# A two-layer encoder on one core: the first projection of each mixer has its weights split 1024 columns at a time instead of 512

## The chip, the cores and the metric

The kernel runs on one core of a Trainium2 chip. The metric is the device time of one execution in microseconds (us), lower is better; the figure for a kernel is the median of its runs.

## What is computed

256 tokens of width 1024 go through two layers. Each layer is a half-weighted SwiGLU feed-forward, a mixer, and a second feed-forward, each added to the stream:

```python
for layer in range(DEPTH):                       # DEPTH = 2
    h = rms_norm(x, ffn1_norm[layer])
    x = x + 0.5 * swiglu(h, ffn1_w_gate[layer], ffn1_w_up[layer], ffn1_w_down[layer])
    h = rms_norm(x, mix_norm[layer])
    if layer % 2 == 0: x = x + even_mixer(h, ...)
    else:              x = x + odd_mixer(h, ...)
    h = rms_norm(x, ffn2_norm[layer])
    x = x + 0.5 * swiglu(h, ffn2_w_gate[layer], ffn2_w_up[layer], ffn2_w_down[layer])
return rms_norm(x, final_norm)
```

The even mixer makes one projection of 1536 columns: queries, keys and values of `a` (8 query heads, 2 key heads, global attention with normed queries and keys and a two-axis rotation) and of `b` (the same sizes, a window of 128 tokens, a one-axis rotation, a sink). The odd mixer projects to queries, keys and values of 16 heads of 64 and attends in a neighbourhood with a learned bias. Each mixer ends with an output projection. All inputs and outputs are float32.

## The kernel before

The program is written out as one ordered list of instructions: each engine (PE, ScalarE = ACT, VectorE = DVE, GpSimd = POOL, SyncE = SP) executes its instructions in the order in which the Python code issues them. There are six stages, numbered 0 to 5: feed-forward, even mixer, feed-forward, feed-forward, odd mixer, feed-forward.

**Weights.** A weight block is loaded by SP as float32 into one of a few `raw` buffers (128x4x512 or 128x2x1024). On the chip it is cut into a high part and a low part of the narrower float type fp32r: `hi` is a copy on ACT (line 482, `high_part`), `lo` is raw minus `hi` on DVE (line 485, `low_part`). Activations are cut in the same way (`th`, `tl`; `oT..h`, `oT..l`; `qTb`, `kTbz` and so on, on the same two lines). A product of 512 columns is then three matmuls: high by high (L474), low by high (L475), high by low (L476).

**Splits.** One raw block becomes two `Split` objects of two pieces of 512 columns each. `Split.step` says how many pieces one `hi` and one `lo` instruction treat: one if the split is `narrow` (128x512), otherwise both (128x1024). The fifth entry that a unit of the plan yields (`"narrow"` or `"wide"`) sets this. The split tiles of weights come from a pool of seven pairs of 128x2x512.

**Order.** After each group of three matmuls `mm` calls `tick`:

```python
def tick(self, supply=True):
    self.low()                        # the lo of the split part whose hi was issued last
    for task in list(self.tasks): ... # small tasks: softmax, transposes, rotations
    if supply:
        self.due += self.rate
        n = self.whole[0].step() if self.whole else 1
        if self.due >= n and self.room():
            self.due = min(self.due - n, n)
            self.supply()             # one hi of the next split, on ACT
```

So `hi` and `lo` of weights to come are strewn between the small tasks of the mixer, at a rate per projection (`EVEN_RATE`, `ODD_RATE`), and a wide split is issued when twice as much is due. The splits issued while one projection is multiplied are those of weights used later. A task counts ticks of `mm`, and the waits between its steps are numbers in tables. A load of the next raw block is issued with the last `lo` of a block.

**The tasks around the change.** In the even mixer, `keys` (L1195 to L1206) turns a key block on PE into a `tp` bank of PSUM (two banks in turn), from which `kTaz`/`kTbz` (ACT, high) and `kTax`/`kTbx` (DVE, low) are made. `queries` rotates on DVE (`t` L1144, `qr` L1157), turns `qr` on PE into the next `tp` bank (L552), and makes `qTb` highs on ACT (L482), then lows on DVE (L485). Scores are matmuls on lines 1068 and 1069, maxima L1081, exponentials `p` L1108, their transposes L1130, copies `pt` L1028, value products `o` L1053. The output projection multiplies `oTa10h`, `oTa10l` (even) or `ot_12h`, `ot_12l` (odd) with split weights, and L617 adds the result to `x`.

Of the kernel before, what the change touches and what calls it, by code (L numbers as in the profile page):

```python
# [21 lines left out]
D = 1024  # L22
# [175 lines left out]
def pairs(stage):  # L198
    return [({"p": "plain", "s": "strassen"}[o[0]], int(o[1:])) for o in DOWN[stage].split()]
# [9 lines left out]
class Trunk:  # L209
# [88 lines left out]
    def plan(self):  # L298


        a = self.a

        def columns(w2d, spans, units=None, kind="narrow"):
            w = sum(n for _, n in spans)
            k = 0
            for nk in units or (4, 4):
                pieces, o = [], 0
                for c0, n in spans:
                    src = w2d[k * P : (k + nk) * P, c0 : c0 + n].rearrange("(k p) n -> p k n", p=P)
                    pieces.append(((slice(0, P), slice(0, nk), slice(o, o + n)), src))  # L310
                    o += n
                yield pieces, nk, w, [2], kind
                k += nk

        def ffn(n, l, stage):
            c0 = 0
            for ci, w in enumerate(FF_CHUNKS):
                first = stage == 0 and c0 == 0
                if ci in SEVEN[stage]:
                    for k in range(0, KD, 2):  # L320
                        pieces = []
                        for i, name in enumerate(("_w_gate", "_w_up")):
                            src = a[n + name][l][k * P : (k + 2) * P, c0 : c0 + w].rearrange("(k p) n -> p k n", p=P)
                            pieces.append(((slice(0, P), slice(0, 2), slice(i * w, i * w + w)), src))
                        yield pieces, 2, D, [2], "strassen" if k >= KD - 2 * SEVEN[stage][ci] else "wide"
                    c0 += w
                    continue
                yield from columns(a[n + "_w_gate"][l], [(c0, w)], FIRST if first else None, "narrow" if first else "wide")
                yield from columns(a[n + "_w_up"][l], [(c0, w)], None, "wide")
                c0 += w  # L330
            for k in range(0, KD, 4):
                pieces = []
                for i, name in enumerate(("_w_gate", "_w_up")):
                    src = a[n + name][l][k * P : (k + 4) * P, c0 : c0 + FF_MIXED].rearrange("(k p) n -> p k n", p=P)
                    pieces.append(((slice(0, P), slice(0, 4), slice(i * FF_MIXED, (i + 1) * FF_MIXED)), src))
                yield pieces, 4, 2 * FF_MIXED, [2], "wide"
            for i, (kind, pair) in enumerate(pairs(stage)):
                src = a[n + "_w_down"][l][2 * pair * P : 2 * (pair + 1) * P, :].rearrange("(k p) n -> p k n", p=P)
                uses = [2, 3 if stage == 5 and i >= len(pairs(stage)) - HELD else 2]
                yield [(slice(0, P), src)], 2, D, uses, "wide" if kind == "plain" else kind  # L340

        def even():
            w_in, w_out = a["even_w_in"][0], a["even_w_out"][0]
            for spans in ([(512, 256), (1280, 256)], [(768, 512)], [(0, 512)]):
                yield from columns(w_in, spans)
            for g in (1, 0):
                for nh in range(2):
                    pieces = []
                    for s in range(2):
                        r0 = g * 512 + s * 256  # L350
                        src = w_out[r0 : r0 + 256, nh * 512 : nh * 512 + 512].rearrange("(j p) n -> p j n", p=HD)
                        pieces.append((slice(64 * s, 64 * s + 64), src))
                    yield pieces, 4, 512, [2], "narrow"

        def odd():
            w_qkv, w_out = a["odd_w_qkv"][0], a["odd_w_out"][0]
            for g in range(2):
                for i in (1, 0, 2):
                    yield from columns(w_qkv, [(i * D + g * 512, 512)])
            for g in range(2):  # L360
                for nh in range(2):
                    src = w_out[g * 512 : g * 512 + 512, nh * 512 : nh * 512 + 512].rearrange("(j p) n -> p j n", p=P)
                    yield [(slice(0, P), src)], 4, 512, [2], "narrow"

        yield from ffn("ffn1", 0, 0)
        yield from even()
        yield from ffn("ffn2", 0, 2)
        yield from ffn("ffn1", 1, 3)
        yield from odd()
        yield from ffn("ffn2", 1, 5)  # L370

# [1207 lines left out]
```

## Time and profile before

| | |
|---|---|
| median of 3 runs | 936.25 us (936.07 to 936.27) |
| the profiled execution | 935.71 us |
| its span on the core | 933.7 us, so 2.0 us lie around it |
| granted TensorE clock | 0.999 of full speed |
| `lo` (L485) and `hi` (L482) of weights | 372 each, 377.7 us on DVE and 320.1 us on ACT |

The even mixer's projections, attention and output projection lie between 180 and 280 us of the span, the odd mixer's between 620 and 760. In the rows of the timeline the first number is the start and the second the time for all instructions of the row; a bracket at the end is how long the engine stood idle before, and for whom. In the windows, numbers follow as busy time and count of PE, weight loads, DVE, ACT and POOL, then the granted clock, the DMA share and GB/s.

### The profile page before, as it was taken

What the parts mean: (1) busy time and instruction counts of PE and PEld (TensorE: products, weight loads), DVE (VectorE), ACT (ScalarE), POOL (GpSimd) and SP (SyncE); (2) the same over time, 40 slices, a digit from 0 to 9 for tenths busy, and PEclk for the clock granted to TensorE, in tenths of its full rate; (3) what the DMA queues carried; (4) which work ended last, traced back from release to release, by engine and by line L of the source; (5) the groups of instructions that cost most, each with busy time, mean ns of one, the idle gap of its engine ahead of it and who ended that gap; (6) DMA issues with size and microseconds to landing.
All of it is one profiled execution on the core that took longest, in us unless ns stands there. A gap on an engine that the chain in (4) does not pass through costs nothing.

```text
span 933.7 us, 12374 instructions
## 1 busy us (share of the span) xinstructions
PE 921.5 (99%) x4405; PEld 754.3 (81%) x4405; DVE 773.4 (83%) x1198; ACT 675.9 (72%) x1084; POOL 92.6 (10%) x152
## 2 busy tenths in 40 slices
PE   9999999999999999999999999999999999999997
PEld 6887888877778888888888888888878888888885
DVE  6799679778868889799878888978867696977898
ACT  7778876467777778885657879657777586778853
POOL 1300000064420000000100000008030000000001
PEclk9999999999999999999999999999999999999999
DMA  8857865644327577757466787566434367588651
GB/s 297 283 172 256 244 213 184 218 142 109 112 92 231 173 237 236 233 191 265 156 193 211 216 278 207 225 210 200 155 99 159 105 204 225 168 265 254 164 212 53
DMA packets 129341, 183.14 MB, mean 196 GB/s; under 512 B 50688, under 2 KB 63744, under 8 KB 129280
## 3 DMA queue, kind: packets, MB, share of 16 engines
q1 hardware_dynamic: 128704, 181.58, 61.8%
q8 instruction: 34, 0.56, 0.2%
q10 hardware_dynamic: 576, 0.79, 0.2%
q14 instruction: 27, 0.22, 0.1%
HBM read 169.76 MB, written 1.05 MB: 183 GB/s over the span
## 4 chain that ended last, share of the span: by engine, by line
PE 88%; DVE 7%; ACT 3%; issue 1%; POOL 0%; POOLq 0%; ACTq 0%; DVEq 0%
PE s L476 13%; PE s L475 13%; PE s L474 12%; PE pj L474 12%; PE pj L475 11%; PE pj L476 11%; DVE lo L485 3%; PE o L474 2%; PE o L476 2%; PE o L475 2%; PE o L1053 2%; PE tp L1130 1%; ACT hi L482 1%; PE tp L530 1%; PE tp L474 1%
## 5 line engine op out<-in xcount | busy, mean ns | idle before, releaser
L485 DVE TENSOR_TENSOR lo<-raw,hi 128x1024 fp32r<-128x1024 f32 (+1 forms) x372 | 377.7, 1034 | 81.8 <-ACT hi L482 80.2
L482 ACT ACTIVATE hi<-raw 128x1024 fp32r<-128x1024 f32 (+1 forms) x372 | 320.1, 892 | 53.9 <-PE s L476 12.6
L474 PE MATMUL s<-hi,th 128*128 128x512 f32 x378 | 148.1, 392 | 0.0
L475 PE MATMUL s<-lo,th 128*128 128x512 f32 x378 | 147.2, 389 | 0.2 <-DVE lo L485 0.2
L476 PE MATMUL s<-hi,tl 128*128 128x512 f32 x378 | 147.2, 390 | 0.0
L474 PE MATMUL pj<-hi,th 128*128 128x512 f32 x366 | 146.2, 399 | 0.0
L475 PE MATMUL pj<-lo,th 128*128 128x512 f32 x366 | 143.2, 391 | 0.6 <-DVE lo L485 0.4
L476 PE MATMUL pj<-hi,tl 128*128 128x512 f32 x366 | 142.8, 390 | 0.0
L475 PEld LDWEIGHTS s<-lo,th 128*128 128x128 f32 x378 | 71.0, 188 | 15.0 <-DVE lo L485 0.5
L476 PEld LDWEIGHTS s<-hi,tl 128*128 128x128 f32 x378 | 70.9, 188 | 14.9
L474 PEld LDWEIGHTS s<-hi,th 128*128 128x128 f32 x378 | 71.0, 188 | 14.5
L475 PEld LDWEIGHTS pj<-lo,th 128*128 128x128 f32 x366 | 68.9, 188 | 15.2 <-DVE lo L485 2.6
L476 PEld LDWEIGHTS pj<-hi,tl 128*128 128x128 f32 x366 | 68.7, 188 | 14.5
L474 PEld LDWEIGHTS pj<-hi,th 128*128 128x128 f32 x366 | 68.8, 188 | 14.0 <-issue 1.0
L494 POOL TENSOR_TENSOR rstd<-var,mhalf 128x1 f32<-128x1 f32 (+2 forms) x16 | 17.1, 1070 | 586.6 <-ACT th L515 309.7
L563 ACT COPY turned<-glu 128x1024 uint16<-128x1024 uint16 (+1 forms) x48 | 60.2, 1253 | 13.2 <-DMA glu<-turned 13.2
L559 ACT COPY turned<-glu 128x1024 uint16<-128x1024 uint16 (+1 forms) x48 | 46.3, 965 | 24.1 <-DVE glu L797 16.3
L482 ACT ACTIVATE shi<-raw 128x1024 fp32r<-128x1024 f32 x28 | 29.6, 1059 | 32.7 <-DVE raw L398 23.0
L474 PE MATMUL s<-hi,g_h 128*128 128x512 f32 (+1 forms) x134 | 52.5, 392 | 0.0
L476 PE MATMUL s<-hi,g_l 128*128 128x512 f32 (+1 forms) x134 | 52.0, 388 | 0.0
L475 PE MATMUL s<-lo,g_h 128*128 128x512 f32 (+1 forms) x134 | 52.0, 388 | 0.0
L482 ACT ACTIVATE shi<-two 128x1024 fp32r<-128x1024 f32 x28 | 29.6, 1058 | 23.8 <-DVE two L398 23.7
(350 smaller groups left out, 1657.3 us busy)
## 6 DMA issues: line engine op xcount, KB each, us to landing
raw<-in_ffn_w_down SPq DMA_DIRECT2D x44, 1024.0 KB, 5.1
raw<-in_ffn_w_up SPq DMA_DIRECT2D x28, 1024.0 KB, 5.1
raw<-in_ffn_w_gate SPq DMA_DIRECT2D x26, 1024.0 KB, 5.3
raw<-in_ffn_w_gate SPq DMA_DIRECT2D x35, 512.0 KB, 4.2
raw<-in_ffn_w_up SPq DMA_DIRECT2D x32, 512.0 KB, 5.2
raw<-in_odd_w_qkv SPq DMA_DIRECT2D x12, 1024.0 KB, 5.2
raw<-in_even_w_in SPq DMA_DIRECT2D x4, 1024.0 KB, 5.1
raw<-in_even_w_out SPq DMA_DIRECT2D x8, 512.0 KB, 5.7
```

Source lines behind the costliest of these rows:

```text
L474: mm(ps, h, wh, start=first, stop=False)
L475: mm(ps, h, wl, start=False, stop=False)
L476: mm(ps, l, wh, start=False, stop=last)
L482: self.nc.scalar.activation(hi, src, AF.Copy)
L485: self.nc.vector.tensor_tensor(lo, src, hi.bitcast(F32), op=ALU.subtract)
L494: nc.gpsimd.tensor_tensor(r[:, :n], v[:, :n], self.mhalf[:, :n], op=ALU.pow)
L530: nc.tensor.transpose(tb[:, j * P : (j + 1) * P], self.x[tt][:, b * P : (b + 1) * P], self.ident)
L559: self.nc.scalar.copy(planes.rearrange("p (h c) -> p h c", h=2), back.rearrange("p (c h) -> p h c", h=2))
L563: self.nc.scalar.copy(planes.rearrange("p (c h) -> p h c", h=2), back.rearrange("p (h c) -> p h c", h=2))
L1053: self.nc.tensor.matmul(O[64 * s : 64 * s + 64, i * P : i * P + P], v(b0 + i, s, kc), pT[s][:, i, kc, :], start=(kc == 0), stop=(kc == 1),)
L1130: nc.tensor.transpose(tb[:, o : o + P], p[:, i, kc * P : kc * P + P], self.ident)
```

## The change

The first projection of each mixer (in the even mixer the keys and values of `a` and `b`, 512 columns in all; in the odd mixer the first keys) gets the kind `"wide"`: its four splits are made by one `hi` and one `lo` of 128x1024 each, instead of two and two of 128x512. The others stay narrow.

```diff
         def even():
             w_in, w_out = a["even_w_in"][0], a["even_w_out"][0]
-            for spans in ([(512, 256), (1280, 256)], [(768, 512)], [(0, 512)]):
-                yield from columns(w_in, spans)
+            for spans, kind in (([(512, 256), (1280, 256)], "wide"), ([(768, 512)], "narrow"), ([(0, 512)], "narrow")):
+                yield from columns(w_in, spans, None, kind)
...
             for g in range(2):
                 for i in (1, 0, 2):
-                    yield from columns(w_qkv, [(i * D + g * 512, 512)])
+                    yield from columns(w_qkv, [(i * D + g * 512, 512)], None, "wide" if (g, i) == (0, 1) else "narrow")
```

PE's and POOL's instructions keep their order. On ACT and DVE each mixer has four `hi` and four `lo` fewer, and since a wide split waits until two pieces are due, those behind the first projection stand elsewhere among the tasks, until the following feed-forward. Three places follow; the number behind a name is a running one, so the same tile may carry another number after the change.

DVE before, from the rotated queries of `b` (first token block) to their low halves, with the keys of the other token block between:

```order
L1157 TENSOR_TENSOR qr_438_2003<-t1_8_439_2004,t2_8_440_2005 128x4x64 x2
L485 TENSOR_TENSOR kTax0_376_1760<-tp_434_1991,kTaz0_374_1758 64x128
L485 TENSOR_TENSOR kTax1_377_1761<-tp_434_1991,kTaz1_375_1759 64x128
L485 TENSOR_TENSOR lo_436_1994<-raw_370_1738,hi_435_1993 128x512
L485 TENSOR_TENSOR kTbx0_380_1766<-tp_441_2018,kTbz0_378_1764 64x128
L485 TENSOR_TENSOR kTbx1_381_1767<-tp_441_2018,kTbz1_379_1765 64x128
L485 TENSOR_TENSOR lo_445_2043<-raw_400_1852,hi_444_2042 128x512
L485 TENSOR_TENSOR qTb00_446_2049<-tp_443_2037,qTb00_446_2049 64x512
L485 TENSOR_TENSOR qTb01_447_2050<-tp_443_2037,qTb01_447_2050 64x512
```

ACT before, at the same place:

```order
L482 ACTIVATE kTaz0_374_1758<-tp_434_1991 64x128
L482 ACTIVATE kTaz1_375_1759<-tp_434_1991 64x128
L482 ACTIVATE hi_435_1993<-raw_370_1738 128x512
L482 ACTIVATE kTbz0_378_1764<-tp_441_2018 64x128
L482 ACTIVATE kTbz1_379_1765<-tp_441_2018 64x128
L482 ACTIVATE hi_444_2042<-raw_400_1852 128x512
L482 ACTIVATE qTb00_446_2049<-tp_443_2037 64x512
L482 ACTIVATE qTb01_447_2050<-tp_443_2037 64x512
L482 ACTIVATE hi_444_2042<-raw_400_1852 128x512
```

DVE after:

```order
L1157 TENSOR_TENSOR qr_439_2000<-t1_8_440_2001,t2_8_441_2002 128x4x64 x2
L485 TENSOR_TENSOR lo_443_2009<-raw_394_1810,hi_442_2008 128x512
L485 TENSOR_TENSOR kTax0_376_1755<-tp_437_1992,kTaz0_374_1753 64x128
L485 TENSOR_TENSOR kTax1_377_1756<-tp_437_1992,kTaz1_375_1754 64x128
L485 TENSOR_TENSOR lo_443_2009<-raw_394_1810,hi_442_2008 128x512
L485 TENSOR_TENSOR kTbx0_380_1761<-tp_444_2019,kTbz0_378_1759 64x128
L485 TENSOR_TENSOR kTbx1_381_1762<-tp_444_2019,kTbz1_379_1760 64x128
L485 TENSOR_TENSOR lo_449_2048<-raw_394_1810,hi_448_2047 128x512
L485 TENSOR_TENSOR qTb00_446_2043<-tp_445_2035,qTb00_446_2043 64x512
L485 TENSOR_TENSOR qTb01_447_2044<-tp_445_2035,qTb01_447_2044 64x512
```

ACT after:

```order
L482 ACTIVATE kTaz0_374_1753<-tp_437_1992 64x128
L482 ACTIVATE kTaz1_375_1754<-tp_437_1992 64x128
L482 ACTIVATE hi_442_2008<-raw_394_1810 128x512
L482 ACTIVATE kTbz0_378_1759<-tp_444_2019 64x128
L482 ACTIVATE kTbz1_379_1760<-tp_444_2019 64x128
L482 ACTIVATE hi_442_2008<-raw_394_1810 128x512
L482 ACTIVATE qTb00_446_2043<-tp_445_2035 64x512
L482 ACTIVATE qTb01_447_2044<-tp_445_2035 64x512
L482 ACTIVATE hi_448_2047<-raw_394_1810 128x512
```

On DVE one `lo` moved up between `qr` and `kTax`. The rows from `kTbx` on read alike, but the `lo` ahead of the `qTb` lows belongs to a `hi` (`hi_448`) that ACT now issues behind the two `qTb` highs, where before it was `hi_444`'s first, ahead of them.

ACT before, at the end of the even mixer, from the last copies `pt` to the output projection's operand `oTa10h`, with the first weights of the following feed-forward (128x1024):

```order
L1028 ACTIVATE pt_649_2820<-tp_647_2808 128x512
L1108 ACTIVATE p_650_2822,sums_623_2721<-s_631_2751,m2_641_2790,by1_583_2579 128x256 x2
L1108 ACTIVATE p_653_2841,sums_623_2721<-s_624_2722,m2_639_2786,by1_583_2579 128x256 x2
L482 ACTIVATE oTa10h_655_2851<-o_652_2832 128x256
L482 ACTIVATE hi_658_2864<-raw_566_2511 128x1024
```

ACT after:

```order
L1028 ACTIVATE pt_649_2812<-tp_648_2804 128x512
L1108 ACTIVATE p_650_2814,sums_625_2717<-s_633_2747,m2_644_2790,by1_584_2575 128x256 x2
L482 ACTIVATE hi_652_2821<-raw_546_2430 128x1024
L1108 ACTIVATE p_655_2837,sums_625_2717<-s_626_2718,m2_642_2786,by1_584_2575 128x256 x2
L482 ACTIVATE oTa10h_657_2847<-o_654_2828 128x256
```

DVE before, at the same place:

```order
L1120 RECIPROCAL r_651_2825<-sums_623_2721 128x2
L1120 RECIPROCAL r_654_2844<-sums_623_2721 128x2
L617 SCALAR_TENSOR_TENSOR x0_84<-pj_607_2667,x0_84 128x512
L485 TENSOR_TENSOR oTa10l_656_2852<-o_652_2832,oTa10h_655_2851 128x256
L485 TENSOR_TENSOR lo_659_2865<-raw_566_2511,hi_658_2864 128x1024
```

DVE after:

```order
L1120 RECIPROCAL r_651_2817<-sums_625_2717 128x2
L485 TENSOR_TENSOR lo_653_2822<-raw_546_2430,hi_652_2821 128x1024
L1120 RECIPROCAL r_656_2840<-sums_625_2717 128x2
L617 SCALAR_TENSOR_TENSOR x0_84<-pj_609_2664,x0_84 128x512
L485 TENSOR_TENSOR oTa10l_658_2848<-o_654_2828,oTa10h_657_2847 128x256
```

The wide `hi` moved from behind `oTa10h` to ahead of the last `p`, and its `lo` from behind `oTa10l` to ahead of the last reciprocal and of `x`.

DVE before, at the end of the odd mixer:

```order
L617 SCALAR_TENSOR_TENSOR x0_84<-pj_1635_7261,x0_84 128x512
L485 TENSOR_TENSOR lo_1651_7334<-raw_1600_7106,hi_1650_7333 128x1024
L617 SCALAR_TENSOR_TENSOR x0_84<-pj_1636_7262,x0_84 128x512
L485 TENSOR_TENSOR ot1_12l_1656_7356<-o_1654_7342,ot1_12h_1655_7355 128x256
L485 TENSOR_TENSOR lo_1661_7374<-raw_1600_7106,hi_1660_7373 128x1024
```

DVE after:

```order
L485 TENSOR_TENSOR ot1_10l_1648_7302<-o_1644_7279,ot1_10h_1647_7301 128x256
L485 TENSOR_TENSOR lo_1650_7309<-raw_1599_7079,hi_1649_7308 128x1024
L617 SCALAR_TENSOR_TENSOR x0_84<-pj_1637_7250,x0_84 128x512
L617 SCALAR_TENSOR_TENSOR x0_84<-pj_1638_7251,x0_84 128x512
L485 TENSOR_TENSOR lo_1658_7343<-raw_1599_7079,hi_1657_7342 128x1024
L485 TENSOR_TENSOR ot1_12l_1656_7340<-o_1654_7326,ot1_12h_1655_7339 128x256
```

The wide `lo` behind `ot1_12l` now stands ahead of it, and its `hi` (ACT) stands directly behind `ot1_12h`.

On SP a load of `odd_w_qkv` stands one place ahead among the loads of the relative bias, and a load of gate weights ahead of a transposing transfer in the last feed-forward.

## The prediction

> **What bounds the kernel now.** I read the page's busy shares first, then the windows of the two mixers, then the waits of PE there, and last the timeline row by row around each wait.
>
> ```profile
> span 933.7 us, 12374 instructions
> PE 921.5 (99%) x4405; PEld 754.3 (81%) x4405; DVE 773.4 (83%) x1198; ACT 675.9 (72%) x1084; POOL 92.6 (10%) x152
> ...
> L485 DVE TENSOR_TENSOR lo<-raw,hi 128x1024 fp32r<-128x1024 f32 (+1 forms) x372 | 377.7, 1034 | 81.8 <-ACT hi L482 80.2
> L482 ACT ACTIVATE hi<-raw 128x1024 fp32r<-128x1024 f32 (+1 forms) x372 | 320.1, 892 | 53.9 <-PE s L476 12.6
> ```
>
> TensorE is busy 921.5 of 933.7 us. Less work on DVE or ACT shows in the time only where PE stands idle, and PE has 12.2 us of idle in all. The change touches the two mixers, so the question is how much of the idle lies there, and behind whom. The windows give, per stretch, its length and then busy time (and count) of PE, weight loads, DVE, ACT and POOL:
>
> ```profile
> 205.00:215.00 10.00, 8.75 (x48) 6.77 (x47) 9.58 (x22) 6.77 (x17) 4.58 (x13) 1.00 0.73 163
> 215.00:225.00 10.00, 9.03 (x55) 7.12 (x53) 9.07 (x24) 7.80 (x25) 5.36 (x12) 1.00 0.47 107
> 245.00:265.00 20.00, 19.56 (x133) 15.70 (x132) 16.40 (x39) 14.71 (x39) 8.00 (x14) 1.00 0.23 79
> ```
>
> Of 20 us at 205 to 225, PE loses 1.25 + 0.97 = 2.22, and DVE is busy 9.58 and 9.07 of 10 there: this is the one place where DVE, not PE, sets the pace. At 245 to 265 it loses 0.44. The longest waits of PE between 175 and 300, and the only one between 600 and 780 (total, times, longest):
>
> ```profile
> PE s L1068 <- ACT p L1108: 1.0, 1, 1.0
> PE tp L552 <- DVE kTax L485: 0.7, 1, 0.7
> PE s L1068 <- DVE qTb L485: 0.6, 1, 0.6
> ```
>
> ```profile
> PE tp L1130 <- ACT pt L1028: 0.5, 1, 0.5
> ```
>
> None of these is a matmul waiting for a `lo` of weights: the splits run ahead of their use. What PE waits for is a small result (a key half, a query half) that stands in DVE's queue. So the place of each `lo` in that queue matters more than its length.
>
> **What is removed.** Per mixer, eight `hi` and eight `lo` of 128x512 become four and four of 128x1024; with both mixers that is eight instructions fewer on each engine. Prices: a `lo` of 128x512 is 0.69, of 128x1024 1.22; a `hi` is 0.63 and 1.08 (rows below). Each merged pair saves 2 x 0.69 - 1.22 = 0.16 on DVE and 2 x 0.63 - 1.08 = 0.18 on ACT: 1.3 and 1.4 us of engine time in all. PE does not wait for these weights, so I book 0. Without this cover it would be worth at most 1.3 + 1.4 = 2.7 us. The loads on SP keep their order but for a projection load that passes some loads of the relative bias, and one of gate weights that passes a transpose; PE's waits above hold none on a transfer, and I book 0.
>
> **What is moved.** The merging leaves every later `hi`/`lo` of the mixer at another place among its neighbours, although PE's order is the same. The rows that bear on the even mixer's first queries, DVE, ACT and PE apart:
>
> ```profile
> 200.86 0.69 DVE L485 TENSOR_TENSOR lo<-raw,hi 128x512 fp32r<-128x512 f32 x1 [0.40 <-ACT hi L482]
> ...
> 204.29 1.53 DVE L1144 SCALAR_TENSOR_TENSOR t<-pj,rstd,tab 128x512 f32<-128x512 f32 x3
> 205.86 1.03 DVE L1157 TENSOR_TENSOR qr<-t,t 128x256 f32<-128x256 f32 x2
> 206.81 0.58 DVE L485 TENSOR_TENSOR kTax<-tp,kTaz 64x128 fp32r<-64x128 f32 x2
> 207.42 0.69 DVE L485 TENSOR_TENSOR lo<-raw,hi 128x512 fp32r<-128x512 f32 x1
> 208.14 0.59 DVE L485 TENSOR_TENSOR kTbx<-tp,kTbz 64x128 fp32r<-64x128 f32 x2
> 208.76 0.69 DVE L485 TENSOR_TENSOR lo<-raw,hi 128x512 fp32r<-128x512 f32 x1
> 209.49 1.41 DVE L485 TENSOR_TENSOR qTb<-tp,qTb 64x512 fp32r<-64x512 f32 x2
> ```
>
> ```profile
> 206.09 0.63 ACT L482 ACTIVATE hi<-raw 128x512 fp32r<-128x512 f32 x1
> 208.20 1.20 ACT L482 ACTIVATE qTb<-tp 64x512 fp32r<-64x512 f32 x2 [1.48 <-PE tp L552]
> 209.43 0.63 ACT L482 ACTIVATE hi<-raw 128x512 fp32r<-128x512 f32 x1
> ```
>
> ```profile
> 207.54 0.63 PE L552 MATMUL tp<-mats,qr 128*128 128x128 f32 x4 [0.69 <-DVE kTax L485]
> ...
> 210.23 0.39 PE L1068 MATMUL s<-kTbz,qTb 128*128 128x256 f32 x1 [0.57 <-DVE qTb L485]
> ```
>
> Step 1, the keys' turn. A `lo` now stands between `qr` and `kTax`. PE's transposes of `qr` (207.54) need the bank that `kTax` reads and ended its last wait 0.15 after `kTax`. Does DVE reach `qr` earlier in exchange? Between the keys' `ssq` and `t` there is one `lo` fewer, but one more stands ahead of `ssq`, and its `hi` is done by ACT only behind the square that `ssq` waits for. What can be won is the 0.40 idle ahead of 200.86, what can be lost some 0.2, by which that `lo` is later than the idle was long. I take `t` to start at 204.29 as now. Price: one `lo` back to back, 207.42 to 208.14 less gaps, 0.61 to 0.69; I take **+0.62**. Bounds: 0.62 - 0.4 and 0.69 + 0.2, so 0.2 and 0.9.
>
> Step 2, the queries' low half. Before, the `lo` at 208.76 uses the `hi` of 206.09, done well before ACT turns to the two `qTb` highs. After, the `lo` in that place uses a `hi` that ACT issues behind both highs. So the first low half, which needed only its own high (end about 208.79), now waits for: second high, end 209.40; `hi`, 0.63; `lo`, 0.69; gaps of some 0.05. Counted from the same transposes its start goes from 209.49 to 209.43 + 0.63 + 0.04 + 0.69 + 0.03 = 210.82: **+1.33**, on top of step 1. The scores at 210.23 read it, and nothing stands between on PE that could cover more. The trace has this very structure once already, at the second row of tokens:
>
> ```profile
> 219.20 0.63 ACT L482 ACTIVATE hi<-raw 128x512 fp32r<-128x512 f32 x1
> ```
>
> ```profile
> 219.87 0.69 DVE L485 TENSOR_TENSOR lo<-raw,hi 128x512 fp32r<-128x512 f32 x1 [0.19 <-ACT hi L482]
> 220.59 1.41 DVE L485 TENSOR_TENSOR qTb<-tp,qTb 64x512 fp32r<-64x512 f32 x2
> ```
>
> ```profile
> 221.42 0.36 PE L1068 MATMUL s<-kTbz,qTb 128*128 128x256 f32 x1 [0.96 <-ACT p L1108]
> ```
>
> There `hi`, `lo`, low half and scores follow head to tail, and PE loses 0.96 (put down to `p`, which ended before the low half at about 221.3 did). In the changed kernel this place keeps its order, so its loss stays and is not counted. Bounds of step 2: 0.7 (the `lo` alone) and 1.5. The `ssq` and POOL's key chain behind it start about a `hi` and a `lo` later (1.3); PE turns those keys only behind the `qr` transposes, which step 1 delays too, and no wait of PE names them. I book 0 (up to 0.3).
>
> Step 3, the end of the even mixer. A `hi` of 128x1024 now stands on ACT ahead of the last exponentials `p`, and its `lo` ahead of their reciprocal. Rows of ACT, DVE and PE:
>
> ```profile
> 267.19 0.40 ACT L482 ACTIVATE oTa10h<-o 128x256 fp32r<-128x256 f32 x1
> 267.45 1.08 ACT L482 ACTIVATE hi<-raw 128x1024 fp32r<-128x1024 f32 x1
> ```
>
> ```profile
> 267.81 0.69 DVE L617 SCALAR_TENSOR_TENSOR x<-pj,x 128x512 f32<-128x512 f32 x1 [0.24 <-issue]
> 268.42 0.41 DVE L485 TENSOR_TENSOR oTa10l<-o,oTa10h 128x256 fp32r<-128x256 f32 x1
> 268.75 1.22 DVE L485 TENSOR_TENSOR lo<-raw,hi 128x1024 fp32r<-128x1024 f32 x1
> ```
>
> ```profile
> 269.19 0.39 PE L476 MATMUL pj<-hi,oTa10l 128*128 128x512 f32 x1
> ```
>
> The two `p` move back by the wide `hi`, about 1.05, and so does `oTa10h`, from 267.19 to 268.25. On DVE the wide `lo` (till about 268.4) and the reciprocal of the late `p` now precede `x` and `oTa10l`; with 0.15 for the reciprocal, 0.69 and 0.41, `oTa10l` ends near 269.65 instead of 268.83. PE wants it at 269.19: **+0.5** (0 to 0.8).
>
> Step 4, the end of the odd mixer. A wide `lo` now stands ahead of `ot_12l`:
>
> ```profile
> 743.82 0.42 DVE L485 TENSOR_TENSOR ot_12l<-o,ot_12h 128x256 fp32r<-128x256 f32 x1 [1.06 <-ACT ot_12h L482]
> 745.37 1.23 DVE L485 TENSOR_TENSOR lo<-raw,hi 128x1024 fp32r<-128x1024 f32 x1 [1.13 <-ACT hi L482]
> ```
>
> ```profile
> 746.35 0.39 PE L476 MATMUL pj<-hi,ot_12l 128*128 128x512 f32 x1
> ```
>
> Its `hi` can start behind `ot_12h` at 743.8: 1.05, then 1.23, then 0.42 makes 746.5 against the 746.35 at which PE wants it: **+0.15** (0 to 0.3). The other places, 225 to 265 and the odd mixer's first queries, change `lo` positions without a wait I can name: 0 (-0.4 to +0.4).
>
> Sum: 0.62 + 1.33 + 0.5 + 0.15 = 2.6 us. The profiled execution took 935.71 and would take 938.3; it lies 0.54 under the median 936.25, so the forecast in the terms of the median is 936.25 + 2.55, about **938.8**. The terms' bounds add up to 936.8 and 940.2; as they will hardly all end on one side, its own range is 937.6 to 939.8. From no change this measurement can tell about 0.2%, 1.87 us: 934.38 to 938.12.
>
> **The rivals.** First, the delay is paid but given back. PE's 2 us pause at 208 to 212 lets ACT and DVE, which lag there, catch up, and the 0.97 lost at 215 to 225 shrinks or goes; the end of the even mixer has its 0.36 of cover (268.83 against 269.19) and more. Then 1.95 - 0.97 to 1.95 - 1.95 remains: 936.3 to 937.3, no change. For it: DVE is the pace there, at 9.58 of 10. Against: the pause at 221.42 starts from PE's own transposes and runs through ACT and DVE anew, whatever was done before.
>
> Second, faster: engine time, not place, decides. DVE and ACT lose 2.7 us of work, the stretches at 205 to 225 are bound by them, and the 2.22 idle closes. From this it would be 936.25 - 2.2 to - 1.0, 934.0 to 935.2; the point of decision is whether the `lo` in front of the `qTb` lows still finds its `hi` ready. Against: the eight pairs lie before 204 and 645, where PE does not wait. [...]
>
> Third, worse: the same order trouble also in the odd mixer, whose queries go through the same steps. If its first scores lose a second 1.33, or its one wait on `pt`, 0.5, doubles, it is 939.6 to 941. Against: the order of `hi`, high, `lo`, low at the odd queries is as before.
>
> **How the numbers follow.** Steps 1 to 4 as worked out: 0.50, of which 0.05 under 938.12. Given back: 0.30. Faster by length: 0.09, of which 0.06 under 934.38. Worse: 0.11. So slower 0.45 + 0.11 = 0.56, same 0.05 + 0.30 + 0.03 = 0.38, faster 0.06. The range from 936.2 to 940.0 leaves out the faster case and about 0.08 of the worse: 0.17.
>
> **What would show it.** Step 1: the wait of `tp` L552 on `kTax` grows from 0.7 to about 1.3. Step 2: the wait of the first scores on `qTb` grows from 0.6 to about 1.9, with `hi` and `lo` head to tail before it. Step 3: a new wait of `pj` L476 on `oTa10l` of about 0.5. Step 4: one of 0.15 on `ot_12l`. PE's busy time in 205 to 215 falls from 8.75 to about 7. The prediction is wrong if these waits are there but later ones vanish, if DVE reaches `t` well before 204.2, or if the first projection's wide splits come too late and PE waits for them near 185.

## The result and the profile after

The changed kernel takes 943.06 us (942.28 to 943.16, 4 runs) against 936.16 us of the kernel before (935.84 to 936.27, 4 runs): a ratio of 1.0072, 95% interval 1.0059 to 1.0084. It is slower by 6.9 us where 2.6 was forecast, and lies outside the range. Built and run again (e5 below) it took 942.02 (941.26 to 942.63, 5 runs) against 935.95, where one of the 15 executions of the kernel before, at 2044.62 us, counts as slow and is left out of the ratio. The profiled execution is one of 943.06. Executions also differ ahead of anything that is changed, mainly at 71 and 181 us, in and behind the first feed-forward: at 200 us PE of the changed kernel is 0.27 us early against the trace of before, and in the traces of the experiments below it is up to 2.4 late.

The page of the changed kernel:

```profile
span 940.7 us, 12370 instructions
...
PE 923.2 (98%) x4405; PEld 755.0 (80%) x4405; DVE 774.1 (82%) x1190; ACT 674.9 (72%) x1076; POOL 92.2 (10%) x152
```

PE is idle 17.5 us instead of 12.2, which is 5.3 of the 7.0 us by which the span grew; and it is busy 1.7 us longer with the same 4405 instructions, so some of them ran slower. PE's waits over the span, changed kernel (total, times, longest):

```profile
PE s L1068 <- DVE qTb L485: 3.2, 2, 2.0
PE o L1500 <- DVE zeros L1494: 1.4, 1, 1.4
PE tp L552 <- DVE kTax L485: 1.4, 1, 1.4
PE tp L530 <- DVE x L617: 1.3, 2, 0.8
...
PE pj L474 <- DVE x L617: 0.4, 1, 0.4
...
PE pj L474 <- DVE t L1142: 0.3, 1, 0.3
```

The second row is the start of the kernel and is there before, too. The waits on `qTb` and `kTax` are those of steps 1 and 2; the waits on `x` and `t` are new. The rows behind steps 1 and 2, DVE, ACT and PE:

```profile
206.59 0.77 DVE L485 TENSOR_TENSOR lo<-raw,hi 128x512 fp32r<-128x512 f32 x1
207.28 0.58 DVE L485 TENSOR_TENSOR kTax<-tp,kTaz 64x128 fp32r<-64x128 f32 x2
...
210.57 0.69 DVE L485 TENSOR_TENSOR lo<-raw,hi 128x512 fp32r<-128x512 f32 x1 [1.38 <-ACT hi L482]
211.30 1.41 DVE L485 TENSOR_TENSOR qTb<-tp,qTb 64x512 fp32r<-64x512 f32 x2
```

```profile
208.68 1.21 ACT L482 ACTIVATE qTb<-tp 64x512 fp32r<-64x512 f32 x2 [2.22 <-PE tp L552]
209.91 0.63 ACT L482 ACTIVATE hi<-raw 128x512 fp32r<-128x512 f32 x1
```

```profile
208.01 0.63 PE L552 MATMUL tp<-mats,qr 128*128 128x128 f32 x4 [1.43 <-DVE kTax L485]
...
212.13 0.35 PE L1068 MATMUL s<-kTbz,qTb 128*128 128x256 f32 x1 [1.99 <-DVE qTb L485]
```

The `lo` stands ahead of `kTax`; high, `hi`, `lo`, low half follow head to tail, as forecast. Set against the trace of before, PE's same instruction is 0.27 early ahead of this place, 0.47 late at 208.01 (+0.74) and 1.90 late at 212.13 (+1.43). What follows was not forecast. Windows of the changed kernel; the number ahead of the DMA share is the granted clock:

```profile
210.00:212.00 2.00, 0.14 (x2) 0.00 (x0) 1.38 (x2) 1.93 (x5) 0.00 (x0) 1.00 0.01 2
212.00:213.00 1.00, 0.87 (x6) 0.77 (x7) 0.69 (x1) 0.30 (x1) 0.00 (x0) 0.78 0.00 0
213.00:214.00 1.00, 1.00 (x4) 0.89 (x4) 0.64 (x1) 0.00 (x0) 0.00 (x0) 0.50 0.00 0
214.00:215.00 1.00, 1.00 (x4) 0.72 (x3) 0.97 (x4) 0.67 (x1) 0.55 (x2) 0.50 0.00 0
215.00:216.00 1.00, 1.00 (x5) 0.81 (x3) 0.34 (x2) 0.99 (x3) 0.54 (x2) 0.51 0.00 0
216.00:217.00 1.00, 1.00 (x8) 0.88 (x8) 0.26 (x1) 1.00 (x6) 0.00 (x0) 1.00 0.61 82
```

Right behind the idle stretch the granted clock is one half for some 3.5 us (212.5 to 216.0), and PE's matmuls of 512 columns take 0.63 apiece instead of 0.40 (0.40 again at 217.29):

```profile
214.51 0.63 PE L474 MATMUL pj<-hi,th 128*128 128x512 f32 x1
```

This costs 1.5: PE is 3.44 late behind it. From there PE's lateness grows to 3.86 by 232 (before's time), 4.49 by 255, 6.25 by 290, and then only at 448 (+0.7) and 746 (+0.11), to 7.05 at the end. Two of the places between 232 and 290 stand in these rows. At the first, a `hi` stands on ACT ahead of the last exponentials (it stood behind them), so the reciprocal and, behind it on DVE, the rotation `t` are late, which frees PE's `pj` bank:

```profile
239.43 0.62 ACT L482 ACTIVATE hi<-raw 128x512 fp32r<-128x512 f32 x1
239.95 0.47 ACT L1108 ACTIVATE p<-s,m 128x256 f32<-128x256 f32 x1
```

```profile
243.29 0.47 PE L474 MATMUL pj<-hi,oTb00h 128*128 128x512 f32 x1 [0.32 <-DVE t L1142]
```

At the second, the entry of the next feed-forward, a wide `lo` stands ahead of `tl` and of the last sums `x` and waits for its `hi`, so `x` comes at 284.98 where 277.79 plus PE's lateness would have made 282.9:

```profile
282.80 1.23 DVE L485 TENSOR_TENSOR lo<-raw,hi 128x1024 fp32r<-128x1024 f32 x1 [1.21 <-ACT hi L482]
283.94 1.12 DVE L520 SCALAR_TENSOR_TENSOR tl<-tp,mats,th 128x128 fp32r<-128x128 f32 x4
284.98 1.28 DVE L617 SCALAR_TENSOR_TENSOR x<-pj,x 128x512 f32<-128x512 f32 x2
```

```profile
285.71 0.66 PE L530 MATMUL tp<-mats,x 128*128 128x128 f32 x4 [0.81 <-DVE x L617]
```

### The profile page after: what moved, and what is told of

Its sections match the earlier page's. It is cut to its first block, busy times and chain, and to the rows that moved or that the text cites. A ratio compares the mean times of both kernels' runs of the same rounds, so it can differ in the third digit from the quotient of the medians.

```text
span 940.7 us, 12370 instructions
## 1 busy us (share of the span) xinstructions
PE 923.2 (98%) x4405; PEld 755.0 (80%) x4405; DVE 774.1 (82%) x1190; ACT 674.9 (72%) x1076; POOL 92.2 (10%) x152
## 4 chain that ended last, share of the span: by engine, by line
PE 75%; DVE 12%; ACT 7%; DMA 3%; issue 2%; POOL 0%; POOLq 0%; ACTq 0%; SPq 0%; DVEq 0%
PE s L475 11%; PE s L476 11%; PE s L474 11%; PE pj L474 10%; PE pj L475 10%; PE pj L476 10%; DVE lo L485 5%; ACT hi L482 2%; PE o L475 2%; PE o L476 2%; PE o L474 2%; DMA glu<-turned 1%; PE o L1053 1%; PE tp L1130 1%; DVE raw L398 1%
```

## The experiments

The theory (P): all of it comes from the places of `hi` and `lo` among the small tasks, and the half clock from PE's idle. Rivals: the width as such (W), a larger share of the odd mixer (O), length (L), scatter (F), another cause of the half clock (N). The edits are shortened to the lines that matter.

**One mixer at a time.**

```diff
 e1: odd mixer as before       e2: even mixer as before
-... "wide" if (g, i) == (0, 1) else "narrow"      -... ([(512, 256), (1280, 256)], "wide")
+... "narrow"                                      +... ([(512, 256), (1280, 256)], "narrow")
```

> Wide splits for the even mixer's first projection alone. Theory P (place and clock): all but about 0.1 of the loss sits in the even mixer and in what follows from it, so about 942.9 us, with the granted clock at one half for some 3.5 us behind 212 as in the changed kernel. Rival W (width as such costs, in each mixer): about half of the 6.9, so 939.6. Rival O (the odd mixer's share is large): under 941.

Measured 941.12 (940.52 to 943.65, 4 runs); ratio 1.0049 (1.0032 to 1.0066).

> Wide splits for the odd mixer's first projection alone. Theory P: 936.2 to 936.4 us, since the odd mixer's queries keep their order and only the place at its end costs 0.1 to 0.15. Rival W: about 939.6. Rival O: over 938.

Measured 935.90 (935.36 to 936.91, 10 runs); ratio 0.9997 (0.9987 to 1.0006). The odd mixer's half costs nothing that can be told; its profile shows the 0.11 at 746.6. The loss is the even mixer's. The first kernel's median lies 1.8 under the 942.9 expected; the one execution that was profiled took 943.65 and had the half clock (214.0 to 217.4), the other three took 940.5 to 941.1. So not each execution need have it. The record gives a mean granted clock of every execution, and it points the same way: 0.996 for the profiled one, 0.998 for the other three. The losses of the two kernels add up to 4.1 of the 6.9; all four executions of the changed kernel have 0.996 or 0.997, so the half clock goes some way to explain the rest.

**Width or place.** Two kernels set the two apart, each with one line behind the even mixer's first projection:

```diff
                 made[g].append(self.start(keys(g, tt, ps)))
+        self.due -= 0.4      # e3: kernel before, all narrow
+        self.due += 0.45     # e4: changed kernel, both wide
```

> All splits of the mixers narrow as before; behind the even mixer's first projection the count of due pieces is lowered by 0.4, which puts the highs and lows between 204 and 232 us at the places that they have in the changed kernel. No wide instruction is in it. Theory P: the keys' turn loses 0.6 more, the scores 1.4 more, the clock then drops to one half and costs another 1.4; the end of the even mixer keeps the places of before, so 939.5 to 940 us. Rival W: 936.2, since nothing is wide. Rival N (the waits come from the places, but the half clock has another cause): 938.2 with a clock of 1.00 throughout.

Measured 939.67 (938.97 to 940.90, 5 runs); ratio 1.0037 (1.0024 to 1.0050). With no wide instruction in it, the longest waits of PE between 100 and 300 are these:

```profile
PE s L1068 <- DVE qTb L485: 3.2, 2, 2.0
PE tp L552 <- DVE kTax L485: 0.8, 1, 0.8
PE pj L474 <- DVE t L1142: 0.3, 1, 0.3
```

Step 2's wait and the one on `t` are those of the changed kernel; at `kTax` only 0.15 is added, since one `lo` fewer stands ahead of `t`. The clock was 1.00 throughout the profiled execution, with the same wait of 2.0: the half clock is not a matter of this wait alone. The median lies in the expected range, but not by the terms of the expectation: the profiled execution (938.97) lost nothing to the clock, and 0.3 at the second scores and 0.5 at `t` that were not counted. The other four have a mean clock of 0.996 or 0.997 against its 0.999, so that they may have had the half clock; no trace shows it.

> The changed kernel, both first projections wide; behind the even mixer's first projection the count of due pieces is raised by 0.45, which puts the highs and lows from 204 us on back at the places of before, one piece further ahead. Theory P: all losses of the even mixer go, 936.2 to 936.8 us. Rival W: 943 still. Rival L (length decides: eight instructions fewer on DVE and ACT, now without the bad places): 935 or less.

Measured 936.78 (936.40 to 937.96, 10 runs); ratio 1.0005 (0.9996 to 1.0014). With both projections wide and the places restored, the loss is gone; that settles width against place. Nor does the saved engine time show: rival L falls. One wait stays larger than before, since one `lo` more stands ahead of `t`:

```profile
PE tp L552 <- DVE kTax L485: 1.3, 1, 1.3
PE s L1068 <- ACT p L1108: 0.9, 1, 0.9
PE s L1068 <- DVE qTb L485: 0.6, 1, 0.6
```

**The half clock.** Four kernels on one chip:

> The changed kernel unedited, on the chip of the three kernels that follow, as their base: 942.3 to 943.2 us if the half clock comes in every execution; executions near 941.5 among them if it comes only in some.

Measured 942.02 (941.26 to 942.63, 5 runs). The profiled execution (942.02) had the same wait of 2.0 and no half clock; 0.9 of its time is the difference at 71 and 181.

```profile
213.32 0.36 PE L1068 MATMUL s<-kTbz,qTb 128*128 128x256 f32 x1 [1.99 <-DVE qTb L485]
```

```profile
213.00:214.00 1.00, 0.68 (x6) 0.62 (x6) 0.86 (x2) 0.50 (x1) 0.00 (x0) 1.00 0.00 0
214.00:215.00 1.00, 1.00 (x7) 0.87 (x6) 0.70 (x2) 0.00 (x0) 0.00 (x0) 1.00 0.00 0
```

So of two profiled executions of this program one had the half clock (0.50 at 213 to 215, the result's) and one did not (1.00, here).

```diff
 e6, in the changed kernel, ahead of the qr transposes (18) and of the first scores (26):
+    for _ in range(n): nc.tensor.matmul(t[:, :P], self.ident16, self.far[0], start=True, stop=True)
```

> The changed kernel with small matmuls whose result is not used (128 columns, bf16) in PE's two stalls: 18 ahead of the transposes of the first qr, 26 ahead of the first scores. Order and waits of the other engines are the same. Theory I (the half clock behind 212 is set off by PE's idle just before it): the granted clock stays 1.00 there and the time falls by about 1.4 against the changed kernel on this chip, to about 941.6 us. Rival N (the half clock has another cause): clock 0.5 for some 3.5 us as before, time the same or up to 0.5 longer for the added matmuls.

Measured 941.33 (940.98 to 941.73, 5 runs), 0.7 under the changed kernel beside it, where 1.4 was expected for executions with the half clock; the two ranges overlap, and so do the ratios (1.0057, 1.0044 to 1.0070, against 1.0064, 1.0051 to 1.0076), so the difference is not told from none. The windows of its profiled execution, where PE's busy time ahead of the scores rises from 6.58 to 9.07 of 10:

```profile
205.00:215.00 10.00, 9.07 (x80) 7.55 (x79) 8.05 (x18) 5.62 (x12) 4.26 (x11) 1.00 0.48 107
215.00:225.00 10.00, 8.74 (x53) 7.13 (x53) 9.50 (x26) 8.06 (x27) 3.79 (x10) 1.00 0.47 106
```

As the kernel beside it was profiled without the half clock too, and only one of its five executions has a mean clock under 0.998, this fits theory I and does not prove it. The opposite, a longer stall, on another chip:

```diff
 e11, in the changed kernel, ahead of the first query block's lows:
+    nc.vector.memset(d, 0.0)
+    for _ in range(3): nc.vector.tensor_tensor(d, d, d, op=ALU.add)
```

> The changed kernel with a memset and three additions of 128x512 on DVE, on a tile of their own, ahead of the first query block's low halves: PE's stall ahead of the first scores grows from 2.0 to about 4.3 us. Theory I (an idle stretch of PE sets off the half clock for some 3.5 us): the half clock comes in every execution, also in the profiled one, and the time grows by the stall's 2.3 and by 1.4 to 1.7 over executions without it, to about 945.5 us. Rival N: it grows by 2.3 alone, to about 944.2, with the clock at 1.00.

Measured 946.06 (945.91 to 946.56, 4 runs); ratio 1.0108 (1.0095 to 1.0121). PE's wait is 4.71, and behind it the clock falls:

```profile
215.85 0.36 PE L1069 MATMUL s<-kTbz,qTb 128*128 128x256 f32 x1 [4.71 <-DVE qTb L485]
```

```profile
216.00:217.00 1.00, 1.00 (x7) 0.81 (x7) 0.43 (x1) 0.00 (x0) 0.00 (x0) 0.54 0.00 0
217.00:218.00 1.00, 1.00 (x5) 0.81 (x5) 0.72 (x2) 0.00 (x0) 0.00 (x0) 0.50 0.00 0
218.00:219.00 1.00, 1.00 (x4) 0.81 (x3) 0.99 (x4) 0.79 (x1) 0.67 (x2) 0.50 0.00 0
```

In this trace PE falls 1.5 further behind during the half clock. All four executions lie within 0.7 us. The longer wait alone (4.7 - 2.0 = 2.7) would bring the changed kernel's 941.26 to 942.63 (on the other chip) to 944.0 to 945.3; they took 0.6 and more beyond that. Their mean clocks are 0.995 or 0.996, while none of the 52 executions of the kernel before that stand beside e1 to e12 has less than 0.997; 3.5 us at one half lower the mean over 940 us by about 0.002 (an estimate from these figures). So an idle stretch of 4.7 us, behind one of 1.4, was very likely followed by the half clock in all four; one of 2.0 behind 1.4 was in the profiled executions of the changed kernel, e1 and e9, and was not in those of e5 and e10.

**The hold.** No `hi` between the highs and lows of a query block:

```diff
-        yield 1
+        self.hold = True; yield 1; self.hold = False        # in stack_q
-            if self.due >= n and self.room():
+            if self.due >= n and not self.hold and self.room():
```

> The changed kernel, but no high part of weights is issued between the high halves and the low halves of a query block (both mixers), so the low halves follow their highs at once. Theory P: the first scores no longer wait (-1.9), the clock stays at 1.00 (-1.4), the second token block's scores gain about 1.1, so about 938.6 us; what is lost at the keys' turn (0.6) and at the end of the even mixer (1.5) stays. Rival W (width): 943.

Measured 940.31 (938.73 to 941.29, 5 runs), 1.7 under the changed kernel beside it; half of what was expected. Its profiled execution (941.29) was 2.4 late at 200 us already; from there on it loses 3.4, where e5's loses 5.1. The expected 1.4 of the clock could hardly be won, as e5 mostly ran without the half clock. In the trace the wait at the first scores adds nothing over the kernel before any more, and the clock stays at 1.00; the second scores, 0.45 earlier, give 0.53 back three microseconds later, where the transposes of `p` wait for POOL. The rest, on `kTax` (1.4), `t` and `x`, stays, as expected.

> The kernel before with the same hold, all splits narrow. Theory P: the waits of the scores on the query low halves, 0.57 and 0.96 us, go: 934.7 us, faster than before by about 1.5. Rival: the lows are late for another reason (the highs, the bank), and it stays at 936.2.

Measured 934.84 (934.49 to 935.94, 11 runs) against 935.95; ratio 0.9991 (0.9981 to 1.0000), faster than the changed kernel, and than the kernel before at the very edge of what the times can tell. The wait of the first scores stays at 0.57: a `lo` whose `hi` is issued before the highs still precedes their low halves. The second scores start at 220.47 instead of 221.42, since the low halves now precede the `lo`:

```profile
219.73 1.41 DVE L485 TENSOR_TENSOR qTb<-tp,qTb 64x512 fp32r<-64x512 f32 x2
...
221.47 1.29 DVE L485 TENSOR_TENSOR lo<-raw,hi 128x512 fp32r<-128x512 f32 x2
```

Of the 0.99 won there 0.66 is lost at 223.4, again at the transposes of `p`; small gains at 254 and 654 make 0.8 in all.

**Where the later loss sits.** The same 0.45, given later:

```diff
+        self.due += 0.45              # e9: ahead of the even mixer's output projection
+            self.due += 0.45 * (g == "a")   # e10: ahead of the projection of a's queries
```

> The changed kernel, but at the start of the even mixer's output projection the count of due pieces is raised by 0.45: from about 240 us on the highs and lows stand where they stood before; the queries of both kinds keep the changed places. Theory P: what the trace of the changed kernel lost at its counterparts of 265, 268.65 (0.57) and 279.65 (0.95) goes, about 1.8 less than the changed kernel, so 940.2 us against 942.0 on the last chip. Rival W: no change, 942. Rival F (the late losses are scatter of transfers, not places): no change either, but with the waits on x at other places.

Measured 940.91 (938.38 to 941.98, 6 runs); ratio 1.0044 (1.0032 to 1.0056). In its profiled execution PE's lateness does not grow behind 245: the 1.76 at 255 to 290 is gone, by places alone. It had the half clock (214.5 to 218.0), which cost 1.5.

> The changed kernel, with the count of due pieces raised by 0.45 already at the start of the even mixer's last projection (the queries of a): only the first block of queries of b, 204 to 222 us, keeps the changed places. Theory P: the losses of 0.6 and 1.4 there stay, with 0.3 at the second scores, and the half clock in some executions; all later ones go (0.5 at 239, 0.2 at 245, 1.8 at the end), so 938.2 to 938.8 us. Rival W: 942.

Measured 939.25 (938.72 to 939.82, 5 runs); ratio 1.0034 (1.0022 to 1.0046), 0.5 over the expected. In its trace PE loses 0.75 and 1.42 at the first queries and nothing more until 700; the clock was 1.00.

**An earlier hold.** On top of e8, for `b`'s queries the hold begins at the turn of `qr`:

```diff
             tb = self.turned(qr.rearrange("p j s d -> p (j s d)"))
-            yield 1
+            self.hold = g == "b"; yield 1
```

> The kernel before with all splits narrow; no high part of weights is issued between the highs and lows of a query block, and for the queries of b none from the turn of qr on, so that no weight low stands ahead of the first query lows. Theory P: the second scores' 0.96 go as in the kernel with the shorter hold (934.8), and 0.5 more at the first scores: 934.3 us, faster than both kernels by 1.9 and 8. Rival: the later lows pile up behind and take it back, 934.8 to 936.

Measured 935.77 (935.16 to 936.77, 11 runs); ratio 0.9997 (0.9989 to 1.0006). Nothing is won that could be told. No `lo` stands directly ahead of the first lows any more, and the scores wait 0.51 all the same:

```profile
209.25 1.20 ACT L482 ACTIVATE qTb<-tp 64x512 fp32r<-64x512 f32 x2 [2.13 <-PE tp L552]
```

```profile
210.48 1.41 DVE L485 TENSOR_TENSOR qTb<-tp,qTb 64x512 fp32r<-64x512 f32 x2 [0.69 <-ACT qTb L482]
```

DVE stands idle for 0.69 and starts the first low half when both highs have ended (210.45). So the sentence of step 2 that it "needed only its own high" was wrong; the sum of the step did not rest on it, since before, too, the low half started behind both. At the second scores the rival is right in part: two `lo` stand between `qr` and their low halves, where in e8 there is one, and the scores wait 0.49, where in e8 they did not wait:

```profile
219.39 0.90 DVE L485 TENSOR_TENSOR lo<-raw,hi 128x512 fp32r<-128x512 f32 x1
```

```profile
222.14 0.39 PE L1068 MATMUL s<-kTbz,qTb 128*128 128x256 f32 x1 [0.49 <-DVE qTb L485]
```

## Why the prediction was wrong

Its sign was right, and so was the mechanism of the steps that it priced. Steps 1 and 2, 0.62 and 1.33, came as +0.74 and +1.43, at the waits named, by the rows named; e3 gives step 2 (+1.42) without any wide instruction. Step 3, 0.5, came as +0.57 at the same place, though by another wait: the `x` of L617, not `oTa10l`, holds PE up, because `x` frees the `pj` bank. Both stand in the same delayed row of DVE, but that the size agreed is in part luck:

```profile
273.93 0.47 PE L474 MATMUL pj<-hi,oTa10h 128*128 128x512 f32 x1 [0.37 <-DVE x L617]
```

Step 4, 0.15, came as +0.11. These four make 2.85 against 2.6; with the 1.5 of the half clock, 0.4, 0.6 and 1.2 of places not priced, and 0.7 at 448, less the 0.27 by which the trace was early, they are the 7.05 within rounding. The failure is in two other terms.

The first is the line "The other places, 225 to 265 and the odd mixer's first queries, change `lo` positions without a wait I can name: 0 (-0.4 to +0.4)", and the silence on what comes after step 3. Those places cost 0.4 (216 to 232), 0.6 (232 to 255) and, with step 3 taken off, 1.2 (255 to 290), of which 0.95 at the entry of the feed-forward. They are of the kind of steps 2 and 3: a `hi` ahead of exponentials, a `lo` that waits for its `hi` ahead of the last `x`. I had looked at operands with little slack in the trace of before; at these places the slack was larger and the shift larger still. e9 and e10 show that they hang on the places: e9 gets rid of those behind 245, e10 of all of them. This term alone would have been enough to miss the range: in e5, whose profile has no half clock, the fastest execution took 941.26.

The second is that a stall was priced at its own length. The half clock behind it added 1.5 in the profiled execution; the profiles show it in e1 and e9 too, and not in e5 and e10. The rest is 0.7 at 448 in the profiled execution of the changed kernel, where `x` waits behind late weights and transfers (ACT's idle for loads ahead of its `hi` at 441.65 and 445.17 is 3.06 and 1.03, against 2.84 and 0.21 before); e5, the same program, does not have it.

The rival "given back" did not come: the second scores lost another 0.3 instead of gaining, as argued, and nothing later made up for it. The rival by length fell with e4 (936.78 against 936.46): like the changed kernel (1190 instructions on DVE against 1198) it has eight fewer there, and its time is no shorter. The third rival, the odd mixer, fell with e2. The range ended at 940.0 because the worse case was tied to the odd mixer, not to more places like those found.

## What to carry to other kernels

Where one engine is the bound at 99% and others feed it in strict order, a change of an instruction's width can change the order of all that follows; go through every place of the shifted order, with the sum of the shift and not with the slack of the old trace, until the order is the same again. A count that is spent in larger steps leaves another remainder, and it can be put right by one line, as e4 shows. Keep filler work from standing between the two halves of a result that the bound engine waits for: the hold, which does this, took 934.84 against 935.95 in e8 and 940.31 against 942.02 in e7.

## What the runs showed of the hardware

A wait of PE of 2.0 us, with another of 1.4 ahead of it, was followed in some profiled executions by 3.5 us at a granted clock of one half (the changed kernel, 212.5 to 216.0; e1; e9), which cost 1.5 us in the changed kernel's and in e9's, and in others by none (e5, e10). One of 4.7 us was followed by it in the one execution profiled (e11, 216.0 to 219.5), with all four executions alike in time and in their mean clock (0.995 or 0.996). The kernel before, whose longest wait there is 0.96, did not show it in its profile, and none of its 52 executions beside e1 to e12 has a mean clock under 0.997. What length of idle PE can have without the half clock, these runs do not show.
